# Differential-attention q and k stored in rows of four and loaded as one DMA of 128 rows; Hyena with its own buffers for both parts, its loads issued first, its pointwise work on VectorE alone

## The chip, the cores and the metric

The kernel runs on one core of one Trainium2 chip. Its time is the device time of one execution in microseconds (us). Three runs of the kernel before lie between 4696.3 and 4708.67, with a median of 4706.38.

## The reference

Two backbone layers work on a trunk of 1024 latent tokens and 256 context tokens, 1024 channels, everything in fp32. A layer is: adaLN RMSNorm, one input projection whose columns go to four head groups, the four mixers, concatenation and output projection with a gated residual, then a squared-ReLU MLP. The context stream is needed after layer 0 only, so layer 1 computes the output for the latent tokens alone. The four mixers are gated DeltaNet (a chunked recurrence), Hyena, HGRN2 (a chunked recurrence with vector gates) and differential attention. Two of them are touched here:

```python
def hyena_mixer(...):                       # per stream: 1024 latent tokens, 256 context tokens (layer 0 only)
    v, x1, x2 = _split(conv_centred(t, conv_w), [W_GROUP] * 3)
    z = x1 * long_conv_bidir(v, h_fwd0, h_bwd0, skip[0])     # order 0; a convolution by FFT over 2n
    return x2 * long_conv_bidir(z, h_fwd1, h_bwd1, skip[1])  # order 1
# differential attention: two softmax maps per head over q, k of 32 channels each
# out = (softmax(q1 k1) - lam * softmax(q2 k2)) @ v, then a sub-norm
```

## The kernel before, in words

**Stages of a layer.** Norm; projection (TensorE bound) with the DeltaNet woven in; HGRN2 with the end of the projection and the start of Hyena woven in; attention with the rest of Hyena, the modulation vectors (`mods`) and, in layer 0, the filters of layer 1 woven in; then the tail (output projection and MLP), which is almost all TensorE. The weaving is done by Python generators: `mix(lead, fill)` takes a step of the lead (HGRN2 in `hgrn`, later attention), which yields its size, and then as many steps of the fill (`rest`) as that size pays for. What comes earlier in that order has priority; a planner then orders each engine's instructions by priority among those that its own clock thinks ready. Each engine, and the queue SP that issues nearly all DMAs, runs its list strictly in order. A tile with one buffer can be written again only when all readers of the old contents are done, and a new memory pool waits for the readers of what lay at its place.

**Where Hyena starts.** `rest` (inside `run`) ends the projection, frees the pools on the right side of the memory (normed activations, weights, projection temporaries), opens attention's pool, issues the q and k loads of the first head (`next(at[0])`, L1157), issues the first two loads of modulation weights (`next(m2)`, L341), and only then starts `hyena`, whose first loads are its own (L1446 to L1458, the DFT bases through `basis`, L1311). All of that is issued before HGRN2's next tile (`hg_tile`) issues its loads (L1033 to L1041).

**Hyena.** The long convolution is done as two DFTs by matmul. In layer 0 the part "c" (256 context tokens, radix R = 2, one block, a = 1) runs first and then the part "l" (1024 latent tokens, R = 4, a = 2); in layer 1 only "l". Input `u` (yv), gate `xg` (y1 or y2) and spectrum `ks` have one buffer each for both parts, as large as "l" needs. For each order `od`, `u` is transposed (`put`, L1468, TensorE), transformed (`pF`, L1317), multiplied with the spectrum (L1504 to L1509) between radix butterflies (L1497 to L1502 and L1515 to L1525), and transformed back (`py`, L1532) into `u`. Of these pointwise instructions, 6 of an "l" block and 1 of a "c" block go to GpSimd (`G`), the others to VectorE (`V`), with two extra tiles `t1` and `t2`.

**q and k of attention.** They are kept in two halves, a high and a low part that add up to the fp32 value, so that a product needs pairs of parts. `post_d` writes [part, channel, group, token] to scratch, one DMA for each chunk of 512 or 256 tokens, from the tile `dhl` that has one buffer (L654 to L657). `load` in `attn` fills, for each of two maps of a head, 128 partitions for q (high, low, high, low of 32 channels) and 128 for k (high, high, low, low) by two DMAs of 64 partitions each: eight per head, 320 KB each (256 KB for q in layer 1). The heads 1 to 3 are loaded two query tiles into the head before.

Of the kernel before, what the change touches and what calls it, by code (L numbers as in the profile page):

```python
# [9 lines left out]
F32 = mybir.dt.float32  # L10
# [10 lines left out]
CTX = 256  # L21
# [219 lines left out]
class K:  # L241
# [185 lines left out]
    def scratch(self, l):  # L427
        S = self.S = {}
        for n in CM_COL:
            if n in ("hf", "hb"):  # L430
                S["k" + n] = self.dram(f"k{n}_{l}", [128, 2, T])
                S["l" + n] = self.dram(f"l{n}_{l}", [128, T // 64, 2, 2, 64])
            elif n in ("dq", "dk"):
                S[n] = self.dram(f"{n}_{l}", [2, 128, 2, T])
            elif n[0] != "g":
                S[n] = self.dram(f"{n}_{l}", [128, 2, T])
        g = self.dram(f"g_{l}", [128, 6, T])
        S["gk"], S["gv"], S["gq"] = [g[:, 2 * j:2 * j + 2] for j in range(3)]
        for n in list(S):
            for i in range(2):  # L440
                S[n, i] = S[n][:, :, i] if n in ("lhf", "lhb", "dq", "dk") else S[n][:, i]
        S["g"] = g
        for n, a, w in TM:
            S[n] = self.dram(f"{n}_{l}", [128, NT, w])
        for k in range(KT):
            S["o", k] = self.dram(f"o{k}_{l}", [128, T])
# [190 lines left out]
    def post_d(self, l, tp, name, i, u, a, n):  # L637
        nc = self.nc
        u = u[:, a:a + n]
        r = self.inv_norm(tp, u, self.c["bones32"], 1.0 / 32, 32 * EPS)  # L640
        y = self.e(tp, 2, n)
        nw = self.P["dqw" if name == "dq" else "dkw"]
        nc.vector.scalar_tensor_tensor(y, u, nw, r, ALU.mult, ALU.mult)
        if a < SEQ:

            rc, rs = self.e(tp, 1, n), self.e(tp, 3, n)
            nc.sync.dma_start(rc, self.i["c_rcos"][:, a:a + n])
            nc.sync.dma_start(rs, self.i["c_rsin"][:, a:a + n])
            t2 = self.e(tp, 0, n)
            p = self.aux("prope")  # L650
            nc.tensor.matmul(p[:, :n], self.c["rperm"], y, start=True, stop=True)
            nc.vector.tensor_mul(t2, p[:, :n], rs)
            nc.vector.tensor_mul(y, y, rc)
            nc.vector.tensor_add(y, y, t2)  # L654
        hl = tp.tile([128, 2, 512], F32R, tag="lf", name="dhl", bufs=1)
        self.split(hl[:, 0, :n], hl[:, 1, :n], y, lo_eng=nc.vector)
        nc.sync.dma_start(self.S[name, i][:, :, a:a + n].rearrange("x p t -> p x t"), hl[:, :, :n].bitcast(F32))  # L657


    def gdn(self, l):  # L660
# [476 lines left out]
    def attn(self, l, qp):  # L1137
# [8 lines left out]
        def load(i, b):  # L1146

            out = ops[i, b] = []
            for j in range(2):
                r = slice(64 * b + 32 * j, 64 * b + 32 * j + 32)  # L1150
                for nm, n in (("q", 128 * NQ), ("k", T)):
                    t = pools[heads.index((i, b)) % 2].tile([128, T], F32R, tag=f"{nm}{j}", name=f"{nm}{j}")[:, :n]
                    raw = t.bitcast(F32)
                    src = S["d" + nm, i]
                    for x in range(2):
                        v = src[:, r, :n] if nm == "q" else src[x:x + 1, r, :n].to_broadcast([2, 32, n])
                        nc.sync.dma_start(raw[64 * x:64 * x + 64], v)  # L1157
                    out.append(t)

        pools = [qp]  # L1160
# [280 lines left out]
    def hyena(self, l):  # L1441
# [2 lines left out]
        gp = es.enter_context(tc.tile_pool(name=f"hy{l}", bufs=1, side="right", reuse_waits="tile"))  # L1444
        sk = gp.tile([128, 4], F32, tag="sk", name="sk")
        nc.sync.dma_start(sk, self.i["hysk"][l])  # L1446
        V, G = nc.vector, nc.gpsimd
        for nm, tok0, n, a, R in (("c", SEQ, CTX, 1, 2), ("l", 0, SEQ, 2, 4)):
            if (l, nm) not in self.KS:
                continue  # L1450
            tk = slice(tok0, tok0 + n)
            pn = n // R
            bf, bi = self.basis(gp, "f", nm), self.basis(gp, "i", nm)
            u = gp.tile([128, 2, SEQ], F32, tag="u", name="u")[:, :, :n]
            nc.sync.dma_start(u, S["yv"][:, :, tk])
            for od in range(2):
                xg = gp.tile([128, 2, SEQ], F32, tag="xg", name="xg")[:, :, :n]
                nc.sync.dma_start(xg, S["y1" if od == 0 else "y2"][:, :, tk])  # L1458

                ut = gp.tile([128, 2, 4, 256], F32, tag="ut", name="ut")  # L1460
                for ai in range(a):
# [8 lines left out]
                        nc.scalar.copy(ut[:, ai, b0:b0 + 2], pv)  # L1470
                        yield 0.2
                for k in range(a):
                    ks = gp.tile([128, 4, 2, 256], F32, tag="ks", name="ks")[:, :R]
                    nc.sync.dma_start(ks, self.KS[l, nm][:, od, k])
                    X = gp.tile([128, 4, 2, 256], F32, tag="X", name="X")[:, :R]
                    Y = gp.tile([128, 4, 2, 256], F32, tag="Y", name="Y")[:, :R]
                    t1 = gp.tile([128, 4, 256], F32, tag="t1", name="t1")[:, :R]
                    t2 = gp.tile([128, 4, 256], F32, tag="t2", name="t2")[:, :R]

                    def F(b):  # L1480
                        p = self.big("pF").rearrange("p (r c) -> p r c", r=2)
                        for ri in range(2):
                            self.fourier(bf, ut, a, ri, k, b, p[:, ri])
                        return p
                    Z = X
                    if R == 2:
                        nc.scalar.copy(Y[:, 0], F(0))
                        p = F(1)
                        V.tensor_add(X[:, 0], Y[:, 0], p)
                        V.tensor_sub(X[:, 1], Y[:, 0], p)  # L1490
                    else:
                        for b in range(2):
                            nc.scalar.copy(X[:, b], F(b))
                            p = F(b + 2)
                            V.tensor_add(Y[:, 2 * b], X[:, b], p)
                            V.tensor_sub(Y[:, 2 * b + 1], X[:, b], p)
                        G.tensor_add(X[:, 0], Y[:, 0], Y[:, 2])  # L1497
                        V.tensor_sub(X[:, 2], Y[:, 0], Y[:, 2])
                        V.tensor_add(X[:, 1, 0], Y[:, 1, 0], Y[:, 3, 1])
                        V.tensor_sub(X[:, 1, 1], Y[:, 1, 1], Y[:, 3, 0])  # L1500
                        G.tensor_sub(X[:, 3, 0], Y[:, 1, 0], Y[:, 3, 1])
                        G.tensor_add(X[:, 3, 1], Y[:, 1, 1], Y[:, 3, 0])  # L1502
                    yield 1
                    V.tensor_mul(t1, X[:, :, 0], ks[:, :, 0])  # L1504
                    G.tensor_mul(t2, X[:, :, 1], ks[:, :, 1])
                    V.tensor_mul(Y[:, :, 1], X[:, :, 0], ks[:, :, 1])
                    V.tensor_mul(X[:, :, 0], X[:, :, 1], ks[:, :, 0])
                    V.tensor_sub(Y[:, :, 0], t1, t2)
                    V.tensor_add(Y[:, :, 1], Y[:, :, 1], X[:, :, 0])  # L1509
                    if R == 2:  # L1510
                        V.tensor_add(Z[:, 0], Y[:, 0], Y[:, 1])
                        V.tensor_sub(Z[:, 1], Y[:, 0], Y[:, 1])
                    else:
                        c = [t.rearrange("p a c -> p (a c)").rearrange("p (s r c) -> p s r c", s=2, r=2) for t in (t1, t2)]
                        V.tensor_add(c[0][:, 0], Y[:, 0], Y[:, 2])  # L1515
                        G.tensor_add(c[1][:, 0], Y[:, 1], Y[:, 3])
                        V.tensor_sub(c[0][:, 1], Y[:, 0], Y[:, 2])
                        V.tensor_sub(c[1][:, 1], Y[:, 1], Y[:, 3])
                        c1, d1 = c[0][:, 1], c[1][:, 1]
                        G.tensor_add(Z[:, 0], c[0][:, 0], c[1][:, 0])  # L1520
                        V.tensor_sub(Z[:, 2], c[0][:, 0], c[1][:, 0])
                        V.tensor_sub(Z[:, 1, 0], c1[:, 0], d1[:, 1])
                        V.tensor_add(Z[:, 1, 1], c1[:, 1], d1[:, 0])
                        V.tensor_add(Z[:, 3, 0], c1[:, 0], d1[:, 1])
                        V.tensor_sub(Z[:, 3, 1], c1[:, 1], d1[:, 0])  # L1525
# [197 lines left out]
    def run(self):  # L1723
        nc, tc = self.nc, self.tc
        with ExitStack() as es:
# [4 lines left out]
            for l in range(DEPTH):  # L1730
# [10 lines left out]
                with ExitStack() as ls:  # L1741
# [42 lines left out]
                    def rest():  # L1784
                        yield from project
                        rs.close()
                        at.append(self.attn(l, qs.enter_context(pool("daf", side="right"))))
                        next(at[0])
                        with pool("mods", side="right") as mp:
                            m2 = self.mods(l, range(16, 48), mp)  # L1790
                            next(m2)
                            yield from weave(self.hyena(l), m2, RM[l])
                            if full:
                                yield from self.mods(l + 1, range(16), mp)
                        if full:
                            yield from self.filters(l + 1)
# [58 lines left out]
```

## Time and profile before

| | |
|---|---|
| median of three runs | 4706.38 us |
| the profiled execution, its own time | 4706.21 us |
| its span, first to last instruction | 4704.4 us |
| TensorE busy, VectorE busy, GpSimd busy | 4081.9, 2352.6, 1082.8 us |
| mean granted TensorE clock | 0.915 of full speed |

The durations in the rows come from the one profiled execution. A busy time is the sum of an engine's instructions; idle time in front of an instruction stands in square brackets with what ended it. The two layers stand one after the other: HGRN2, attention and Hyena of layer 0 lie from about 750 to 1560 us and those of layer 1 from about 3200 to 3890 us.

### The profile page before, as it was taken

Reading aid. Unit: us, or ns where it says so; the run is one execution under the profiler, and the core shown is the slowest. Engines: PE = TensorE matmul, PEld = TensorE weight load, DVE = VectorE, ACT = ScalarE, POOL = GpSimd, SP = SyncE. Lnnn points to the kernel's source line nnn. Section 1 sums busy time; section 2 is a strip of 40 time slices with the busy share of each in tenths; the row PEclk is TensorE's granted clock in tenths of the full one; section 3 lists DMA queues with packets and bytes.
Section 4 is the critical chain, followed back from the end, with each engine's and each line's share of the span. In section 5 each row is a group of like instructions: output and inputs, shape, how many; then the busy total and the mean of one; then the engine's idle time right before and its main releaser. Section 6 shows DMA issues by size and latency. Waiting matters only on the chain. (4 is left out here: it accounts for less than half of the span.)

```text
span 4704.4 us, 81485 instructions
## 1 busy us (share of the span) xinstructions
PE 4081.9 (87%) x33270; PEld 3290.9 (70%) x33270; DVE 2352.6 (50%) x4599; ACT 1620.4 (34%) x3165; POOL 1082.8 (23%) x1101
## 2 busy tenths in 40 slices
PE   4987999867477799999999987999847788999999
PEld 2866877655355588888888776776635667888887
DVE  7566556647587353222222756456647874322222
ACT  3453413423245342212122554514313464321222
POOL 1121110000121344333333221120001114433333
PEclk7998999877789899999999998899867899999999
DMA  5236633224324421111111326634342234111112
GB/s 194 87 89 169 199 97 111 92 91 145 97 84 147 156 79 50 36 41 36 41 36 49 118 82 159 184 107 124 97 143 71 84 113 145 64 48 49 46 49 88
DMA packets 381355, 458.61 MB, mean 97 GB/s; under 512 B 137108, under 2 KB 244244, under 8 KB 378933
## 3 DMA queue, kind: packets, MB, share of 16 engines
q1 hardware_dynamic: 379156, 448.42, 30.4%
q0 software_dynamic: 1824, 4.98, 0.4%
q8 instruction: 262, 4.29, 0.4%
q14 instruction: 113, 0.92, 0.1%
HBM read 343.81 MB, written 109.48 MB: 96 GB/s over the span
## 5 line engine op out<-in xcount | busy, mean ns | idle before, releaser
L255 POOL TENSOR_TENSOR wlo<-wraw,whi 128x512 fp32r<-128x512 f32 x360 | 478.3, 1334 | 743.3 <-ACT whi L254 739.2
L254 ACT CAST whi<-wraw 128x512 fp32r<-128x512 f32 (+1 forms) x480 | 296.5, 619 | 905.4 <-PE pt L260 757.4
L1597 DVE SCALAR_TENSOR_TENSOR tx<-pt,mod,tx 128x512 f32<-128x512 f32 (+1 forms) x360 | 250.6, 696 | 590.6 <-PE pt L261 590.5
L260 PE MATMUL pt<-fl,whi 128*128 128x512 f32 (+1 forms) x1280 | 475.4, 371 | 0.0
L261 PE MATMUL pt<-fh,wlo 128*128 128x512 f32 (+1 forms) x1280 | 475.4, 371 | 0.0
L259 PE MATMUL pt<-fh,whi 128*128 128x512 f32 (+1 forms) x1280 | 475.1, 371 | 0.0
L261 PE MATMUL pt<-hh,wlo 128*128 128x512 f32 (+1 forms) x1280 | 471.2, 368 | 2.8 <-POOL wlo L255 2.8
L260 PE MATMUL pt<-hl,whi 128*128 128x512 f32 (+1 forms) x1280 | 471.9, 369 | 0.0
L259 PE MATMUL pt<-hh,whi 128*128 128x512 f32 (+1 forms) x1280 | 471.2, 368 | 0.4 <-ACT f L1630 0.4
L1631 DVE TENSOR_TENSOR f<-f 128x512 f32<-128x512 f32 (+1 forms) x160 | 149.3, 935 | 622.9 <-ACT f L1630 619.2
L259 PE MATMUL pproj<-hh,whi 128*128 128x512 f32 (+1 forms) x960 | 372.0, 387 | 7.0 <-ACT u L487 6.4
L260 PE MATMUL pproj<-hl,whi 128*128 128x512 f32 (+1 forms) x960 | 362.0, 377 | 0.0
L261 PE MATMUL pproj<-hh,wlo 128*128 128x512 f32 (+1 forms) x960 | 360.6, 376 | 0.0
L255 POOL TENSOR_TENSOR fl<-f,fh 128x512 fp32r<-128x512 f32 (+1 forms) x160 | 191.5, 1198 | 390.6 <-ACT fh L254 387.0
L260 PEld LDWEIGHTS pt<-fl,whi 128*128 128x128 f32 x1280 | 240.1, 188 | 47.3 <-issue 0.2
L261 PEld LDWEIGHTS pt<-fh,wlo 128*128 128x128 f32 x1280 | 240.1, 188 | 47.1 <-issue 0.5
L259 PEld LDWEIGHTS pt<-fh,whi 128*128 128x128 f32 x1280 | 240.1, 188 | 47.0 <-ACT whi L254 0.2
L261 PEld LDWEIGHTS pt<-hh,wlo 128*128 128x128 f32 x1280 | 241.3, 188 | 44.3 <-POOL wlo L255 4.1
L259 PEld LDWEIGHTS pt<-hh,whi 128*128 128x128 f32 x1280 | 241.3, 189 | 41.0 <-ACT f L1630 0.8
L260 PEld LDWEIGHTS pt<-hl,whi 128*128 128x128 f32 x1280 | 241.3, 189 | 40.3 <-issue 0.2
L259 PEld LDWEIGHTS pproj<-hh,whi 128*128 128x128 f32 x960 | 186.5, 194 | 47.1 <-ACT u L487 8.2
L1199 ACT ACTIVATE p<-psc,mx 128x1280 f32<-128x1280 f32 (+1 forms) x144 | 178.0, 1238 | 120.0 <-DVE mx L1198 71.1
(380 smaller groups left out, 8330.7 us busy)
## 6 DMA issues: line engine op xcount, KB each, us to landing
wraw<-mlp_w SPq DMA_DIRECT2D x296, 256.0 KB
modw<-mod_w SPq DMA_DIRECT2D x80, 512.0 KB
wraw<-w_cm SPq DMA_DIRECT2D x88, 256.0 KB
wraw<-w_out SPq DMA_DIRECT2D x64, 256.0 KB
kv<-kvd SPq DMA_DIRECT2D x40, 256.0 KB
k<-dk SPq DMA_DIRECT2D x32, 320.0 KB
bfl<-c_hyfl SPq DMA_DIRECT2D x4, 2048.0 KB
modw<-mod_w SPq DMA_DIRECT2D x4, 2048.0 KB
```

Source lines behind the costliest of these rows:

```text
L254: (hi_eng or nc.scalar.copy)(hi, src)
L255: (lo_eng or nc.gpsimd).tensor_tensor(lo, src, hi.bitcast(F32), ALU.subtract)
L259: nc.tensor.matmul(ps, wh, xh, start=start, stop=False)
L260: nc.tensor.matmul(ps, wh, xl, start=False, stop=False)
L261: nc.tensor.matmul(ps, wl, xh, start=False, stop=stop)
L1199: nc.scalar.activation(p[j], A, AF.Exp, bias=mx[:, j:j + 1], accum_out=sm[:, j:j + 1])
L1597: nc.vector.scalar_tensor_tensor(xm, p, G[:, m, v:v + 1], xm, ALU.mult, ALU.add)
L1631: nc.vector.tensor_mul(f, f, f)
```

## The change

q and k scratch has the layout [group, channel, 4, token]. `post_d` writes each chunk by two DMAs from the same tile, so that every channel has its four rows in the order in which the tile wants them (q: high, low, high, low; k: high, high, low, low). The load of one map of one head is then one DMA of 32 channels times 4 rows = 128 rows: four per head.

`hyena` has tiles of their own for the two parts (`uc`, `ul`, `xgc`, `xgl`, `ksc`, `ksl`), issues all first loads of both parts before its first `yield 0`, and loads only later spectra and gates in the loop. `rest` starts Hyena's loads first, then attention's, then those of the modulation weights, and yields 1.0 before Hyena's work. No instruction of Hyena is left on GpSimd; `t1` and `t2` are gone and the products are made in `X` and `Y`; two butterfly pairs are joined into instructions of twice the length.

```diff
-                S[n] = self.dram(f"{n}_{l}", [2, 128, 2, T])
+                S[n] = self.dram(f"{n}_{l}", [2, 128, 4, T])
...
-        nc.sync.dma_start(self.S[name, i][:, :, a:a + n].rearrange("x p t -> p x t"), hl[:, :, :n].bitcast(F32))
+        for d in range(2):
+            rows = slice(2 * d, 2 * d + 2) if name == "dq" else slice(d, 4, 2)
+            nc.sync.dma_start(self.S[name, i][:, rows, a:a + n], hl[:, :, :n].bitcast(F32))
...
-                    raw = t.bitcast(F32)
-                    src = S["d" + nm, i]
-                    for x in range(2):
-                        v = src[:, r, :n] if nm == "q" else src[x:x + 1, r, :n].to_broadcast([2, 32, n])
-                        nc.sync.dma_start(raw[64 * x:64 * x + 64], v)
+                    c0 = 64 * b + 32 * j
+                    nc.sync.dma_start(t.bitcast(F32), S["d" + nm, i][c0:c0 + 32, :, :n].rearrange("c r t -> (c r) t"))
...
+        got = {}
+        for nm, tok0, n, a, R in parts:
+            bf = self.basis(gp, "f", nm)
+            u = gp.tile([128, 2, n], F32, tag="u" + nm, name="u")
+            nc.sync.dma_start(u, S["yv"][:, :, tok0:tok0 + n])
+            ks = spectrum(nm, 0, 0, R)
+            bi = self.basis(gp, "i", nm)
+            got[nm] = bf, bi, u, gate(nm, 0, tok0, n), ks
+        yield 0
...
-                        G.tensor_add(X[:, 0], Y[:, 0], Y[:, 2])
+                        V.tensor_add(X[:, 0], Y[:, 0], Y[:, 2])
...
-                        G.tensor_sub(X[:, 3, 0], Y[:, 1, 0], Y[:, 3, 1])
-                        G.tensor_add(X[:, 3, 1], Y[:, 1, 1], Y[:, 3, 0])
+                        V.tensor_sub(X[:, 3, 0], Y[:, 1, 0], Y[:, 3, 1])
+                        V.tensor_add(X[:, 3, 1], Y[:, 1, 1], Y[:, 3, 0])
...
-                    V.tensor_mul(t1, X[:, :, 0], ks[:, :, 0])
-                    G.tensor_mul(t2, X[:, :, 1], ks[:, :, 1])
+                    V.tensor_mul(Y[:, :, 0], X[:, :, 0], ks[:, :, 0])
                     V.tensor_mul(Y[:, :, 1], X[:, :, 0], ks[:, :, 1])
-                    V.tensor_mul(X[:, :, 0], X[:, :, 1], ks[:, :, 0])
-                    V.tensor_sub(Y[:, :, 0], t1, t2)
-                    V.tensor_add(Y[:, :, 1], Y[:, :, 1], X[:, :, 0])
+                    V.tensor_mul(X[:, :, 0], X[:, :, 1], ks[:, :, 1])
+                    V.tensor_mul(X[:, :, 1], X[:, :, 1], ks[:, :, 0])
+                    V.tensor_sub(Y[:, :, 0], Y[:, :, 0], X[:, :, 0])
+                    V.tensor_add(Y[:, :, 1], Y[:, :, 1], X[:, :, 1])
...
-                        V.tensor_add(c[0][:, 0], Y[:, 0], Y[:, 2])
-                        G.tensor_add(c[1][:, 0], Y[:, 1], Y[:, 3])
-                        V.tensor_sub(c[0][:, 1], Y[:, 0], Y[:, 2])
-                        V.tensor_sub(c[1][:, 1], Y[:, 1], Y[:, 3])
-                        c1, d1 = c[0][:, 1], c[1][:, 1]
-                        G.tensor_add(Z[:, 0], c[0][:, 0], c[1][:, 0])
-                        V.tensor_sub(Z[:, 2], c[0][:, 0], c[1][:, 0])
+                        Z = Y
+                        V.tensor_add(X[:, 0:2], Y[:, 0:2], Y[:, 2:4])
+                        V.tensor_sub(X[:, 2:4], Y[:, 0:2], Y[:, 2:4])
+                        V.tensor_add(Z[:, 0], X[:, 0], X[:, 1])
+                        V.tensor_sub(Z[:, 2], X[:, 0], X[:, 1])
+                        c1, d1 = X[:, 2], X[:, 3]
...
-                        next(at[0])
                         with pool("mods", side="right") as mp:
-                            m2 = self.mods(l, range(16, 48), mp)
-                            next(m2)
-                            yield from weave(self.hyena(l), m2, RM[l])
+                            hy, m2 = self.hyena(l), self.mods(l, range(16, 48), mp)
+                            for g in (hy, at[0], m2):
+                                next(g)
+                            yield 1.0
+                            yield from weave(hy, m2, RM[l])
```

## Rows read from the trace of the kernel before

**Rows 1.** The page: busy time of each engine, and the DMA traffic of the span.
```profile
PE 4081.9 (87%) x33270; PEld 3290.9 (70%) x33270; DVE 2352.6 (50%) x4599; ACT 1620.4 (34%) x3165; POOL 1082.8 (23%) x1101
...
DMA packets 381355, 458.61 MB, mean 97 GB/s; under 512 B 137108, under 2 KB 244244, under 8 KB 378933
```
**Rows 2.** Timeline of TensorE, layer 0: start, duration, line, tiles, [idle before <-releaser].
```profile
1062.32 1.13 PE L1468 MATMUL put<-c_ident,u 128*128 128x128 f32 x4 [32.60 <-DMA u<-yv]
...
1210.34 1.96 PE L1468 MATMUL put<-c_ident,u 128*128 128x128 f32 x8 [34.41 <-DMA u<-yv]
```
**Rows 3.** Waits of TensorE, 3395 to 3900: total us, times, longest.
```profile
PE put L1468 <- DMA u<-yv: 46.5, 1, 46.5
...
PE pmod L363 <- DMA modw<-mod_w: 7.2, 1, 7.2
```
**Rows 4.** The queue SP in layer 1: start, time that the issue took, line.
```profile
3411.82 0.55 SPq L1157 DMA_DIRECT2D q<-dq  x1
...
3429.15 11.38 SPq L1157 DMA_DIRECT2D k<-dk  x2
...
3454.25 2.32 SPq L1455 DMA_DIRECT2D u<-yv  x1
...
3470.75 0.52 SPq L1036 DMA_DIRECT2D k<-khb  x1
```
**Rows 5.** Stretches: busy us of each engine, granted clock, DMA share, GB/s.
```profile
820.00:975.00 155.00, 133.13 (x2179) 99.25 (x2178) 96.99 (x265) 64.77 (x140) 2.70 (x7) 0.87 0.31 98
...
3415.00:3445.00 30.00, 18.92 (x342) 13.29 (x330) 11.66 (x36) 8.62 (x20) 0.37 (x2) 0.60 0.14 52
3455.00:3475.00 20.00, 0.00 (x0) 0.00 (x0) 0.00 (x0) 0.00 (x0) 0.00 (x0) 0.50 1.00 301
3475.00:3485.00 10.00, 0.00 (x0) 0.00 (x0) 0.00 (x0) 0.00 (x0) 0.00 (x0) 0.50 0.15 58
20.00:45.00 25.00, 15.50 (x67) 4.94 (x67) 18.65 (x33) 4.08 (x7) 2.95 (x3) 0.80 1.04 396
```
**Rows 6.** The queue SP in layer 0, as rows 4.
```profile
1000.25 0.52 SPq L1157 DMA_DIRECT2D q<-dq  x1
...
1203.91 0.58 SPq L1455 DMA_DIRECT2D u<-yv  x1
```
**Rows 7.** Timeline of VectorE behind the first waits of the layers.
```profile
1067.15 0.69 DVE L1489 TENSOR_TENSOR X<-Y,pF 128x512 f32<-128x512 f32 x1 [2.33 <-PE pF L1317]
...
1070.82 0.41 DVE L1061 TENSOR_TENSOR X<-X,k 128x256 f32<-128x256 f32 x1
...
3488.37 0.43 DVE L1061 TENSOR_TENSOR X<-X,k 128x256 f32<-128x256 f32 x1 [0.42 <-DMA k<-khb]
```
**Rows 8.** VectorE by line and shape: busy us, mean ns | idle before.
```profile
L1506 DVE TENSOR_TENSOR Y<-X,ks 128x1024 f32<-128x1024 f32 x8 | 17.7, 2218 | 0.0
...
L1518 DVE TENSOR_TENSOR t<-Y 128x512 f32<-128x512 f32 x8 | 11.2, 1397 | 0.0
...
L1498 DVE TENSOR_TENSOR X<-Y 128x512 f32<-128x512 f32 x8 | 10.9, 1360 | 0.0
L1496 DVE TENSOR_TENSOR Y<-X,pF 128x512 f32<-128x512 f32 x16 | 10.9, 680 | 0.0
L1508 DVE TENSOR_TENSOR Y<-t,t 128x1024 f32<-128x1024 f32 x8 | 9.7, 1211 | 0.0
...
L1515 DVE TENSOR_TENSOR t<-Y 128x512 f32<-128x512 f32 x8 | 8.3, 1032 | 0.0
...
L1499 DVE TENSOR_TENSOR X<-Y 128x256 f32<-128x256 f32 x8 | 7.5, 938 | 0.0
...
L1523 DVE TENSOR_TENSOR X<-t,t 128x256 f32<-128x256 f32 x8 | 3.3, 412 | 0.0
```
**Rows 9.** The queue SP in the projection, layer 0, as rows 4.
```profile
835.80 4.34 SPq L657 DMA_DIRECT2D dk<-dhl  x2
```

More of the change, by code (lines that the diff above doesn't have):

```diff
@@ L440, in scratch @@
             for i in range(2):
-                S[n, i] = S[n][:, :, i] if n in ("lhf", "lhb", "dq", "dk") else S[n][:, i]
+                S[n, i] = S[n][:, :, i] if n in ("lhf", "lhb") else S[n][i] if n in ("dq", "dk") else S[n][:, i]
         S["g"] = g
@@ L1149, in load @@
             for j in range(2):
-                r = slice(64 * b + 32 * j, 64 * b + 32 * j + 32)
                 for nm, n in (("q", 128 * NQ), ("k", T)):
                     t = pools[heads.index((i, b)) % 2].tile([128, T], F32R, tag=f"{nm}{j}", name=f"{nm}{j}")[:, :n]
-                    raw = t.bitcast(F32)
-                    src = S["d" + nm, i]
-                    for x in range(2):
-                        v = src[:, r, :n] if nm == "q" else src[x:x + 1, r, :n].to_broadcast([2, 32, n])
-                        nc.sync.dma_start(raw[64 * x:64 * x + 64], v)
+                    c0 = 64 * b + 32 * j
+                    nc.sync.dma_start(t.bitcast(F32), S["d" + nm, i][c0:c0 + 32, :, :n].rearrange("c r t -> (c r) t"))
                     out.append(t)
@@ L1446, in hyena, with gate, spectrum @@
         nc.sync.dma_start(sk, self.i["hysk"][l])
[L1447 to L1450, printed above, removed]
+        V = nc.vector
+        parts = [p for p in (("c", SEQ, CTX, 1, 2), ("l", 0, SEQ, 2, 4)) if (l, p[0]) in self.KS]
+        def gate(nm, od, tok0, n):
+            xg = gp.tile([128, 2, n], F32, tag="xg" + nm, name="xg")
+            nc.sync.dma_start(xg, S["y1" if od == 0 else "y2"][:, :, tok0:tok0 + n])
+            return xg
+        def spectrum(nm, od, k, R):
+            ks = gp.tile([128, R, 2, 256], F32, tag="ks" + nm, name="ks")
+            nc.sync.dma_start(ks, self.KS[l, nm][:, od, k])
+            return ks
+        got = {}
[7 more added lines that the diff above has]
+        yield 0
+        for nm, tok0, n, a, R in parts:
             tk = slice(tok0, tok0 + n)
             pn = n // R
-            bf, bi = self.basis(gp, "f", nm), self.basis(gp, "i", nm)
-            u = gp.tile([128, 2, SEQ], F32, tag="u", name="u")[:, :, :n]
-            nc.sync.dma_start(u, S["yv"][:, :, tk])
+            bf, bi, u, xg, ks = got[nm]
             for od in range(2):
-                xg = gp.tile([128, 2, SEQ], F32, tag="xg", name="xg")[:, :, :n]
-                nc.sync.dma_start(xg, S["y1" if od == 0 else "y2"][:, :, tk])
+                if od:
+                    xg = gate(nm, od, tok0, n)
                 ut = gp.tile([128, 2, 4, 256], F32, tag="ut", name="ut")
@@ L1472, in hyena @@
                 for k in range(a):
-                    ks = gp.tile([128, 4, 2, 256], F32, tag="ks", name="ks")[:, :R]
-                    nc.sync.dma_start(ks, self.KS[l, nm][:, od, k])
+                    if od or k:
+                        ks = spectrum(nm, od, k, R)
                     X = gp.tile([128, 4, 2, 256], F32, tag="X", name="X")[:, :R]
                     Y = gp.tile([128, 4, 2, 256], F32, tag="Y", name="Y")[:, :R]
-                    t1 = gp.tile([128, 4, 256], F32, tag="t1", name="t1")[:, :R]
-                    t2 = gp.tile([128, 4, 256], F32, tag="t2", name="t2")[:, :R]
                     def F(b):
@@ L1484, in F @@
                         return p
-                    Z = X
                     if R == 2:
@@ L1500, in hyena @@
                         V.tensor_sub(X[:, 1, 1], Y[:, 1, 1], Y[:, 3, 0])
-                        G.tensor_sub(X[:, 3, 0], Y[:, 1, 0], Y[:, 3, 1])
-                        G.tensor_add(X[:, 3, 1], Y[:, 1, 1], Y[:, 3, 0])
+                        V.tensor_sub(X[:, 3, 0], Y[:, 1, 0], Y[:, 3, 1])
+                        V.tensor_add(X[:, 3, 1], Y[:, 1, 1], Y[:, 3, 0])
                     yield 1
-                    V.tensor_mul(t1, X[:, :, 0], ks[:, :, 0])
-                    G.tensor_mul(t2, X[:, :, 1], ks[:, :, 1])
+                    V.tensor_mul(Y[:, :, 0], X[:, :, 0], ks[:, :, 0])
                     V.tensor_mul(Y[:, :, 1], X[:, :, 0], ks[:, :, 1])
-                    V.tensor_mul(X[:, :, 0], X[:, :, 1], ks[:, :, 0])
-                    V.tensor_sub(Y[:, :, 0], t1, t2)
-                    V.tensor_add(Y[:, :, 1], Y[:, :, 1], X[:, :, 0])
+                    V.tensor_mul(X[:, :, 0], X[:, :, 1], ks[:, :, 1])
+                    V.tensor_mul(X[:, :, 1], X[:, :, 1], ks[:, :, 0])
+                    V.tensor_sub(Y[:, :, 0], Y[:, :, 0], X[:, :, 0])
+                    V.tensor_add(Y[:, :, 1], Y[:, :, 1], X[:, :, 1])
                     if R == 2:
+                        Z = X
                         V.tensor_add(Z[:, 0], Y[:, 0], Y[:, 1])
@@ L1513, in hyena @@
                     else:
-                        c = [t.rearrange("p a c -> p (a c)").rearrange("p (s r c) -> p s r c", s=2, r=2) for t in (t1, t2)]
-                        V.tensor_add(c[0][:, 0], Y[:, 0], Y[:, 2])
-                        G.tensor_add(c[1][:, 0], Y[:, 1], Y[:, 3])
-                        V.tensor_sub(c[0][:, 1], Y[:, 0], Y[:, 2])
-                        V.tensor_sub(c[1][:, 1], Y[:, 1], Y[:, 3])
-                        c1, d1 = c[0][:, 1], c[1][:, 1]
-                        G.tensor_add(Z[:, 0], c[0][:, 0], c[1][:, 0])
-                        V.tensor_sub(Z[:, 2], c[0][:, 0], c[1][:, 0])
+                        Z = Y
[4 more added lines that the diff above has]
+                        c1, d1 = X[:, 2], X[:, 3]
                         V.tensor_sub(Z[:, 1, 0], c1[:, 0], d1[:, 1])
```

## The prediction, written before the changed kernel was run

> **What bounds the kernel now.** I read the page first: TensorE is busy for 4081.9 of 4704.4 us, VectorE for half of them, and the DMA moves 97 GB/s in the mean [rows 1]. TensorE sets the end, so what can be won is where it stands idle. The waits of TensorE in the stretches that the change touches, HGRN2 to attention, come next: one releaser stands above all others, the load of Hyena's input `u`. TensorE waits for it for 32.6 and 34.4 us in layer 0 [rows 2] and 46.5 us in layer 1 [rows 3], 113.5 us in all. TensorE runs its list in order, so HGRN2 or attention, which come behind `put`, stand too: the multiplications of HGRN2's next tile begin on VectorE at 1070.8 and 3488.4 us [rows 7].
>
> Why `u` is late is read from the queue SP and the DMA share. In layer 1 the eight loads of q and k start at 3411.8 us; the last two alone hold SP for 11.4 us, and `u` is issued at 3454.3 us, HGRN2's next `k` at 3470.8 us [rows 4]. From 3415 to 3445 the DMA share is 0.14 at 52 GB/s: some 2 of 16 engines work (0.14 x 16 = 2.2), at 26 GB/s each. Then the wide transfers come, 1.00 and 301 GB/s, and at the end again 0.15 [rows 5]: the two engines that had q and k still have their share of everything issued behind to do, and `u` is complete only with them. So the loads of q and k are slow, they hold the queue, and they delay what comes behind them even after it has been issued. The second wait of layer 0 has one cause more: `u` of part "l" shares its buffer with part "c" and is issued only at 1203.9 us [rows 6], when "c" has been written out.
>
> **Part 1: q and k as 128 rows.** Removed: 32 of 64 load DMAs. The nearest rows for a transfer of 128 rows are the stretches with all engines at work, 301 GB/s (the modulation weights with their short rows among them) and 396 GB/s (activations) [rows 5]. One head in layer 0 is 4 x 640 KB = 2.62 MB: 6.6 to 8.7 us in place of some 45 us of the two engines (2.62 MB at 58 GB/s). [...]
>
> For heads 1 to 3 the transfers lie beside attention, where VectorE is the busier engine, and I cost them at the one wait that they show: 7.2 us for a modulation weight behind q and k [rows 3]. The other end is 0, if that weight is late anyway.
>
> **Part 2: writing four rows.** Added: 22 DMAs of up to 512 KB, 10.0 MB in all, in the projections, where the DMA share is 0.31 [rows 5]; bandwidth hides them. The cost is `dhl`: with one buffer, the next chunk's cast on ScalarE, and what stands behind it there (the copies that empty PSUM for TensorE), waits until both writes are read out. A second write takes its issue and 1.7 us of transfer (512 KB at 301 GB/s), 2.1 us x 22 = 46 us if every one is on the path; two issues with one chunk's wait between them took 4.34 us [rows 9]. No engine waits for these writes now, and the chunks mostly come further apart than that, so I take 4 us. Ends 0 and 46.
>
> **Part 3: own buffers, loads first.** Moved: six loads in layer 1, eleven in layer 0, in front of q and k and of two modulation loads on SP; those of "l" in layer 0 also in front of HGRN2's loads of several tiles. By the tiles' sizes (1 MB here is 10^6 bytes), layer 1 issues 7.34 MB for Hyena, 2.36 MB of q and k, 1.05 MB of modulation weights: 10.75 MB. Layer 0 has 1.57 MB for "c" and the larger q and k as well: 12.58 MB. Hyena's own wait is gone, since its first 3.1 MB (basis and `u`) take 10 us while TensorE still has work. What is late next is HGRN2's next `k`, which stands behind all of this, as it did before.
> - Layer 1: 3411.8 + 10.75 / 0.301 = 3447.5 in place of 3488.4: **40.9 us** [rows 4, 5, 7].
> - Layer 0, first wait: 1000.25 + 12.58 / 0.301 = 1042.1 in place of 1070.8, 28.7 us [rows 5 to 7]. VectorE had done Hyena's first four instructions between 1067.15 and 1070.82 [rows 7], which now come later: less 3.7 us, **25.0 us**.
> - Layer 0, second wait: `u` of "l" has landed long before and nothing else is missing: all of it, **34.4 us**.
>
> I take 301 GB/s because modulation weights are in both; at 396 the first two give 49.4 and 34.8 us less 3.7, 14.7 us more in all (layer 1: 27.1 us, layer 0: 31.8 us of transfer). At the mean of the span see the rivals.
>
> The `yield 1.0` moves one step of fill behind attention in each layer. Layer 1 ends Hyena well before attention, so nothing; in layer 0 the filters of layer 1 already run on after attention, and one step more alone there costs between 0 and some 20 us. I take 3.
>
> **Part 4: no GpSimd.** Undisturbed, 512 elements take VectorE 0.68 us, 1024 take 1.21 and 256 take 0.41 [rows 8]. An "l" block gains instructions of 512 (butterfly), 2 x 256, 1024 (product), one in the inverse butterfly (0.68), and two pairs of 0.68 there, of which three were VectorE's, become two of 1.21 (+0.38): 0.68 + 0.82 + 1.21 + 0.68 + 0.38 = 3.8 us; 8 blocks are 30 us, and two of "c" 1.4. Against that, those that ran beside GpSimd are stretched: L1506 2.22 in place of 1.21, L1518 1.40, L1498 1.36 and L1515 1.03 in place of 0.68, L1499 and its twin 0.94 in place of 0.41 [rows 8]: 1.01 + 0.72 + 0.68 + 0.35 + 1.06 = 3.8 us a block, 31 us. Net +1 us. The ends: +31 if the stretching stays, -10 if VectorE's other instructions and the waits for GpSimd's results gain too. The cover matters, because VectorE is the busier engine in these stretches.
>
> **Sum.** 40.9 + 25.0 + 34.4 + 7.2 = 107.5 us, less 4 + 3 + 1 = 8: 99.5 us. The profiled execution took 4706.2 us, within 0.2 us of the median, so 4706.2 - 99.5 = **4606.7, forecast 4607**.
>
> **The rivals.**
> - A, the forecast: 0.70, its own range 4580 to 4640.
> - B, the second write of each chunk is on the path: 46 us in place of 4, 4649. For it: one buffer, engines in order. Against: DMA share 0.31 and no such wait now. 0.11.
> - C, the change doesn't do what it says, and the new loads of q and k still sit on two engines. Hyena no longer waits, but HGRN2's `k` does: in layer 1 each of the two has 1.18 MB and a sixteenth of 8.39 MB, 1.70 MB at 26 GB/s = 65.5 us, 3477.3: 11 us gained. In layer 0 1.31 + 0.62 MB, 74 us: 7 us lost with the 3.7. With 34.4 and less 8, 30 us: 4676. Against: both sides now lead with 32 or 128. 0.06.
> - D, slower: the block of 10.75 and 12.58 MB in front of HGRN2's loads becomes the wait. At r GB/s it gains 76.6 - 10750 / r in layer 1 and 66.9 - 12580 / r in layer 0, and 34.4 + 7.2 - 8 besides: 177 - 23330 / r, which turns negative below 132 GB/s. At the 97 GB/s of the span [rows 1] it is -63.5 us, 4770. For it: TensorE's list now has HGRN2's tile in front of Hyena's work, so nothing fills the hole. Against: 301 and 396 GB/s where much is queued [rows 5]. 0.06.
> - E, more than forecast: the transfers at 396 GB/s and VectorE freed of 10 us, 4607 - 14.7 - 11 = 4581, and some clock regained (it was granted at half speed in the waits [rows 5]): below 4570 in 0.07.
>
> **How the numbers follow.** The range is 4566 to 4664: it holds A, E's better part and B, and leaves out C, D and some of E. A measurement can't tell less than 0.3% (14 us) from no change. All of A, B, E and nearly all of C are faster by more; a mix of B, C and D's mild form is the same. Faster 0.92, same 0.02, slower 0.06.
>
> **What would show it.** Right: no wait of TensorE for `u<-yv` over 5 us; a DMA share near 1 for 25 to 40 us from the first q and k loads; HGRN2's next multiplication 40 us (layer 1) and 25 to 30 us (layer 0) earlier against the end of the projection; L1506's successor at 1.2 us. Wrong: a share of 0.13 during q and k (C), ScalarE's cast waiting for `dk<-dhl` (B), a wait of HGRN2 for `k` or `lf` longer than 15 us (D), VectorE instructions in Hyena still stretched (part 4).

## The result and the profile after

The changed kernel takes 4598.77 us (median of four runs, 4594.1 to 4605.16), the kernel before, timed beside it, 4704.45: a ratio of 0.9779, 95% interval 0.9766 to 0.9792. The forecast was 4607, faster. The profiled execution took 4594.1 us with a span of 4592.3 us; the granted clock rose from 0.915 to 0.925 in the mean.

The page of the kernel after, to be held against [rows 1]: TensorE's busy time is the same within 3 us, so all but 3 of the 112 us of span that went are idle time. The four rows cost 10 MB of DMA traffic.
```profile
PE 4079.2 (89%) x33270; PEld 3286.2 (72%) x33270; DVE 2336.7 (51%) x4633; ACT 1617.3 (35%) x3165; POOL 1006.1 (22%) x1051
...
DMA packets 387720, 468.56 MB, mean 102 GB/s; under 512 B 137843, under 2 KB 246515, under 8 KB 385300
```
The transposes `put` in the kernel after, by tile, with what TensorE sat idle for before them. The 113.5 us of [rows 2, 3] have become 0.4.
```profile
L1484 PE MATMUL put<-c_ident,u x72: 275/285/489, 1014.2 to 3560.5; 128*128 128x128 f32 x72
its engine sat idle before it (us, times) until:
  ACT wT L1220: 0.9, 2
  DMA u<-yv: 0.4, 1
```
The queue SP of the kernel after in layer 1, which answers to [rows 4]. The four loads of q and k take 0.3 to 0.6 us each where two of before held SP for 11.4 us, and HGRN2's `k` is issued 14 us after the projection's last write (L535), where it was 57 us before (3413.4 to 3470.75). Between the two pairs stand Hyena's loads (3353.2 to 3357.1): although the code asks for Hyena's loads first, the first pair of q and k still goes ahead of them. The line by itself below them is the projection's last write in the kernel before.
```profile
3350.76 0.32 SPq L1156 DMA_DIRECT2D q<-dq  x1
3352.35 0.32 SPq L535 DMA_DIRECT2D v<-tm  x1
3352.76 0.39 SPq L1156 DMA_DIRECT2D k<-dk  x1
...
3357.69 0.60 SPq L1156 DMA_DIRECT2D q<-dq  x1
3358.65 0.33 SPq L1156 DMA_DIRECT2D k<-dk  x1
3359.02 4.87 SPq L341 DMA_DIRECT2D modw<-mod_w  x2
3366.78 0.52 SPq L1039 DMA_DIRECT2D k<-khb  x1
```

```profile
3413.41 0.32 SPq L534 DMA_DIRECT2D v<-tm  x1
```
The stretches that answer to those of q and k in [rows 5], after: busy us of each engine, granted clock, DMA share, GB/s. The block runs at a share of 1.00 and 400 GB/s while TensorE works beside it.
```profile
1020.00:1040.00 20.00, 14.92 (x296) 11.20 (x296) 6.55 (x23) 4.02 (x9) 0.19 (x1) 0.59 1.00 400
...
3360.00:3380.00 20.00, 17.23 (x280) 12.29 (x280) 7.21 (x21) 7.48 (x18) 0.19 (x1) 0.50 1.00 409
```
VectorE after, at HGRN2's next multiplication of each layer, to be held against [rows 7].
```profile
1041.37 0.41 DVE L1064 TENSOR_TENSOR X<-X,k 128x256 f32<-128x256 f32 x1
...
1044.31 0.69 DVE L1502 TENSOR_TENSOR X<-Y,pF 128x512 f32<-128x512 f32 x1 [1.52 <-PE pF L1316]
...
3382.58 0.42 DVE L1064 TENSOR_TENSOR X<-X,k 128x256 f32<-128x256 f32 x1 [0.20 <-DMA k<-khb]
```
And VectorE by line and shape after, against [rows 8]: nothing in Hyena's pointwise work is stretched any more (L1511 here is L1498 there, L1512 is L1499).
```profile
L1518 DVE TENSOR_TENSOR Y<-X,ks 128x1024 f32<-128x1024 f32 x8 | 9.7, 1217 | 0.0
...
L1511 DVE TENSOR_TENSOR X<-Y 128x512 f32<-128x512 f32 x8 | 5.5, 683 | 0.0
...
L1512 DVE TENSOR_TENSOR X<-Y 128x256 f32<-128x256 f32 x8 | 3.3, 417 | 0.0
```

Where the time went, by fixed points of both traces (starts on the queue and on TensorE, us from the span's start; `psc` are attention's scores, `pfin` the transposes that end HGRN2, `pt` the products of the tail):

| stretch | before | after | gained |
|---|---|---|---|
| start to the projection's last write, layer 0 | 999.9 | 1005.8 | -5.9 |
| to attention's first `psc` (HGRN2) | 137.8 | 106.1 | 31.7 |
| to the first `pt` of the tail (attention, Hyena, filters) | 483.4 | 454.0 | 29.4 |
| to the projection's last write, layer 1 | 1792.3 | 1786.5 | 5.8 |
| to the last `pfin` (HGRN2) | 171.8 | 127.6 | 44.2 |
| to the last `psc` (attention) | 281.6 | 269.8 | 11.8 |
| to the last `pt` of the tail | 833.5 | 838.4 | -4.9 |

The gains sum to 112.1 us, which are the 112 us of the spans. The medians differ by 105.7.

### The profile page after: what moved, and what is told of

Read it like the earlier page. It is cut to its first block, busy times and chain, and to the rows that moved or that the text cites. A ratio compares the mean times of both kernels' runs of the same rounds, so it can differ in the third digit from the quotient of the medians.

```text
span 4592.3 us, 81385 instructions
## 1 busy us (share of the span) xinstructions
PE 4079.2 (89%) x33270; PEld 3286.2 (72%) x33270; DVE 2336.7 (51%) x4633; ACT 1617.3 (35%) x3165; POOL 1006.1 (22%) x1051
```

## The experiments

In all of them the ratio is to the kernel before, timed on the same chip beside them.

**q and k alone (e1_qk).** The kernel before with the changed scratch, the doubled writes and the loads of 128 rows, and nothing else of the change.
```diff
-                    for x in range(2):
-                        v = src[:, r, :n] if nm == "q" else src[x:x + 1, r, :n].to_broadcast([2, 32, n])
-                        nc.sync.dma_start(raw[64 * x:64 * x + 64], v)
+                    nc.sync.dma_start(t.bitcast(F32), S["d" + nm, i][c0:c0 + 32, :, :n].rearrange("c r t -> (c r) t"))
```


> The kernel before with the q and k part alone (rows of four, two writes a chunk, one load of 128 rows); Hyena, its order and GpSimd as before. Theory (the two engines are the main cause): in layer 0, 2.62 + 1.05 + 1.05 MB before the gate land in 16 us, in layer 1 9.7 MB in 32 us, so both first waits of TensorE for u shrink to under 8 us; in the second wait of layer 0, u is still issued after part c has been written out, and some 10 of 34 us stay. 4704 - 30 - 42 - 23 - 7 + 6 = about 4608 us, no later than 4625. Rival (order and shared buffers are the main cause): the waits for u stay above 20 us each and the time is 4650 us or more.

Measured: 4585.54 us, ratio 0.973 (0.9702 to 0.9757). This one part brings more than the whole change, and 22 us more than the theory's 4608. `u` still has its one buffer and stands behind q, k and the modulation weights, and yet no wait for it is left. The transposes of this kernel, by tile:
```profile
L1466 PE MATMUL put<-c_ident,u x72: 271/283/465, 1029.6 to 3532.7; 128*128 128x128 f32 x72
its engine sat idle before it (us, times) until:
  ACT wT L1219: 0.5, 1
  ACT ut L1468: 0.4, 2
```

**All but q and k (e2_loads).** The changed kernel with scratch, writes and loads of q and k as before.
```diff
-                    nc.sync.dma_start(t.bitcast(F32), S["d" + nm, i][c0:c0 + 32, :, :n].rearrange("c r t -> (c r) t"))
+                    for x in range(2):
+                        v = src[:, r, :n] if nm == "q" else src[x:x + 1, r, :n].to_broadcast([2, 32, n])
+                        nc.sync.dma_start(raw[64 * x:64 * x + 64], v)
```


> The changed kernel with q and k as before (one write a chunk, eight loads of 64 rows a head); Hyena's own buffers, loads first and no GpSimd stay. Theory (the two engines are the main cause): Hyena no longer waits for u, but HGRN2's next k stands behind q and k on the two engines until 3477 us in layer 1 and 1074 us in layer 0, as it did before; what is gained is the second wait of layer 0 (34 us) and 10 us besides: 4655 to 4675 us. Rival (order and buffers are the main cause): 4620 us or less.

Measured: 4734.58 us, ratio 1.0051 (1.0033 to 1.007): half a per cent slower than before, which neither theory allowed. Hyena's loads now stand ahead of most of q and k, and `u` is still waited for by 15.0 us in layer 0; above all, TensorE waits for what comes last instead, the modulation weights behind q and k. Its waits in layer 0 (990 to 1650) and its queue SP:
```profile
PE pmod L363 <- DMA modw<-mod_w: 72.3, 10, 37.9
...
PE put L1485 <- DMA u<-yv: 15.0, 1, 15.0
```
```profile
1022.09 5.18 SPq L1157 DMA_DIRECT2D k<-dk  x2
1027.31 17.32 SPq L1157 DMA_DIRECT2D q<-dq  x2
1044.68 12.33 SPq L1157 DMA_DIRECT2D k<-dk  x2
1057.05 6.02 SPq L341 DMA_DIRECT2D modw<-mod_w  x1
```
These loads of q and k hold the queue for 35 us (5.2 + 17.3 + 12.3), and the wait has only changed its name: 37.9 us at one `pmod` in layer 0, 37.7 at one in layer 1. Own buffers and early loads do not remove a wait that slow transfers cause. This kernel has the yield too, which costs some 19 to 26 us in the pairs below; how much of its loss is the yield's, no run tells.

**The pointwise work alone (e3_nopool).** The kernel before with Hyena's pointwise instructions on VectorE, made in `X` and `Y`.
```diff
-                    V.tensor_mul(t1, X[:, :, 0], ks[:, :, 0])
-                    G.tensor_mul(t2, X[:, :, 1], ks[:, :, 1])
+                    V.tensor_mul(Y[:, :, 0], X[:, :, 0], ks[:, :, 0])
...
+                    V.tensor_mul(X[:, :, 0], X[:, :, 1], ks[:, :, 1])
```


> The kernel before with the pointwise work of Hyena alone changed (all on VectorE, in place, joined pairs). Theory: VectorE's 31 us more of instructions and 31 us less of stretching cancel: 4700 to 4710 us, with each 1024-element product at 1.21 us. Rival 1: VectorE is the bound there and the added work shows: 4720 us or more. Rival 2: other instructions gain as well: 4690 us or less.

Measured: ratio 0.9986 (0.9972 to 0.9999), 4704.69 us; most likely a gain of 7 us, between 0 and 13 by the interval, hardly told from none.

**Hyena's loads last (e4_last).**
```diff
-                            for g in (hy, at[0], m2):
+                            for g in (at[0], m2, hy):
```


> The changed kernel with the order of the first loads turned round: attention's q and k, then the modulation weights, then Hyena's. Theory: with all engines at work the order no longer matters, since u and the basis still land some 20 us after the first issue, before TensorE runs out of work: within 8 us of the changed kernel's 4599. Rival (loads first is what counts): TensorE waits again for u in front of its first transposes, over 10 us in each layer: 4615 to 4640 us.

Measured: 4597.98 us, ratio 0.9758 (0.9732 to 0.9783). The order of the loads is worth nothing that can be told once q and k are wide.

**Two halves that do not lead with 2 (e5_halves).** The change, with each load cut into two of 64 partitions, 16 channels times 4 rows each, joined into one dimension of 64 rows.
```diff
-                    nc.sync.dma_start(t.bitcast(F32), S["d" + nm, i][c0:c0 + 32, :, :n].rearrange("c r t -> (c r) t"))
+                    for x in range(2):
+                        c1 = c0 + 16 * x
+                        nc.sync.dma_start(t[64 * x:64 * x + 64].bitcast(F32), S["d" + nm, i][c1:c1 + 16, :, :n].rearrange("c r t -> (c r) t"))
```


> The changed kernel with each load of q or k cut into two DMAs of 64 rows (16 channels of four rows each), with a leading dimension of 16 or more instead of the 2 of the kernel before. Theory (the short leading dimension held them on two engines): same time as the changed kernel, 4593 to 4606 us, DMA share near 1 during q and k. Rival (it is the joining of two halves that counts): back to a share near 0.14 and 4650 us or more.

Measured: 4613.38 us, ratio 0.9802 (0.9779 to 0.9826), some 15 us over the change by the medians (11 by the ratios, whose intervals overlap) and 7 over the upper end of the theory, far from the 4650 of the rival. The windows of this kernel, columns as in [rows 5]:
```profile
1000.00:1020.00 20.00, 12.15 (x281) 9.64 (x279) 8.30 (x30) 5.61 (x14) 0.39 (x1) 0.76 0.87 300
1020.00:1040.00 20.00, 12.86 (x270) 9.17 (x268) 6.32 (x22) 4.03 (x9) 0.19 (x1) 0.59 1.03 309
```
Halves as such are not confined to few engines; halves that lead with 2 are. The Trainium skill ("DMA: Bandwidth & Descriptors", section "Rules for kernel authors") says that an outermost dimension of fewer than 16 confines a DMA to at most that many engines. The trace agrees: a leading dimension of 2 left the share at 0.14 [rows 5], and the halves of 64 rows brought it to 1.03. The same section says that two transfers to disjoint halves of the partitions both spread over all 16 engines. That agrees with the halves here (1.03) and not with those of the kernel before (0.14), where the measurement decides.

Most of what remains can be seen as waits for the modulation weights, which stand behind twice as many issues: 15.1 us in layer 0 where the change has 4.5, and 9.3 in layer 1 where it has 1.4.

**Four loads of 32 rows, single write (e6_rows32).** The change with the scratch and the single write of before; each tile is filled by four DMAs of 32 channels.
```diff
+                    for m, x in enumerate((0, 1, 0, 1) if nm == "q" else (0, 0, 1, 1)):
+                        nc.sync.dma_start(raw[32 * m:32 * m + 32], src[x, r, :n])
```


> The changed kernel with the scratch and the single write of a chunk as before, and each map of a head loaded by four DMAs of 32 rows (one part each) instead of one of 128: sixteen issues a head. Theory (leading dimension, and the doubled write costs some 6 us in the projection of layer 0): 4590 to 4600 us, the end of the projection in layer 0 back at 1000 us. Rival 1 (32 rows at a time are slow, or sixteen issues hold the queue): 4610 to 4640 us. Rival 2 (the doubled write costs nothing): 4599 us.

Measured: 4615.96 us, ratio 0.9808 (0.9784 to 0.9833), in the range of the first rival, though its interval overlaps that of the change. The projection of layer 0 ends at 998.2 us where that of the change ends at 1005.8, so the second write seems to cost something there (the mean over all traces is taken below); but four loads of `k` in a row held SP for 10.8 us, the weights were late by 10.1 us, and TensorE was busy for only 7.5 of the 20 us from 1020 to 1040.
```profile
1008.31 10.82 SPq L1156 DMA_DIRECT2D k<-dk  x4
```

**Without the yield (e7_noyield).**
```diff
-                            yield 1.0
```


> The changed kernel without the yield of 1.0 behind the first loads, so that Hyena's first transposes come one step of HGRN2 earlier in the order. Theory: one step of fill less runs alone after attention in layer 0: 0 to 6 us faster, 4593 to 4599. Rival (the step keeps TensorE from waiting for u, or HGRN2 from being held back): TensorE waits for u by 5 to 15 us in a layer and the time is 4605 to 4620.

Measured: 4572.6 us, ratio 0.9713 (0.969 to 0.9737): 26 us faster than the change, where six were the most that was expected. The inverse transform of Hyena's part "l" in layer 0 begins 16 us earlier than in the change (1173.4 for 1189.1), and the last filter multiplication ends the stage 23 us earlier. Counted from the projection's last write, which itself came 3 us earlier, these are 12 and 20 us. The filter multiplications of layer 1 that are woven into layer 0, by tile, from 1400 to 1600 us, first in the change, then in the kernel without the yield:
```profile
L1396 PE MATMUL pw<-wh,h2l x16: 468/696/1096, 1486.3 to 1542.7; 128*128 128x512 f32 x16
```
```profile
L1396 PE MATMUL pw<-wh,h2l x16: 467/700/796, 1460.5 to 1519.5; 128*128 128x512 f32 x16
```
Attention itself ends before that (its last `psc` is at 1468.4 and 1452.8 us), so in layer 0 the fill ends last, and what puts the fill off puts the tail off.

**GpSimd put back (e8_gp).** The change with the six instructions per "l" block and the one per "c" block on GpSimd again, in place.
```diff
-                        V.tensor_add(X[:, 0], Y[:, 0], Y[:, 2])
+                        G.tensor_add(X[:, 0], Y[:, 0], Y[:, 2])
...
-                    V.tensor_mul(X[:, :, 0], X[:, :, 1], ks[:, :, 1])
+                    G.tensor_mul(X[:, :, 0], X[:, :, 1], ks[:, :, 1])
```


> The changed kernel with six instructions of each l block and one of each c block put back on GpSimd, in place as they are now (they run beside VectorE and stretch it). Theory (added work and stretching cancel): 4594 to 4606 us, VectorE instructions beside GpSimd stretched again to 1.4 to 2.2 us, the waits of TensorE for Hyena's products as long as now. Rival 1: GpSimd off is worth something: 4610 us or more. Rival 2: VectorE is the bound: 4585 us or less.

Measured: 4610.47 us, ratio 0.9795 (0.9772 to 0.9819): 12 us more by the medians, at the lower end of the first rival, though the ratio's interval overlaps that of the change. VectorE's instructions are stretched as in [rows 8], and one of them now waits for GpSimd's product:
```profile
L1511 DVE TENSOR_TENSOR X<-Y 128x512 f32<-128x512 f32 x8 | 11.2, 1402 | 0.0
...
L1520 DVE TENSOR_TENSOR X<-X,ks 128x1024 f32<-128x1024 f32 x8 | 9.8, 1223 | 7.5 <-POOL X L1519 7.5
```

**q and k with the pointwise work (e9_qk_pw).** The edits of e1_qk and e3_nopool together: shared buffers, old order, no yield.

> The kernel before with the rows of four for q and k and the pointwise work on VectorE alone: shared buffers, the old order of loads, no yield. It and the change without its yield (4572.6 us) differ in the own buffers and the order of the loads alone. Theory (those are worth nothing once q and k are wide): 4572, within 8 us. Rival (the 13 us between q and k alone, 4585.5, and the change without its yield come from own buffers and early loads, part 4 gives nothing): 4580 to 4590.

Measured: 4565.57 us, ratio 0.9705 (0.9684 to 0.9726), the best of all, and the same as the change without its yield (0.9713). Those two differ in own buffers and early loads alone, so these are worth nothing here. This holds for the second wait of layer 0 too, where `u` of "l" shares its buffer with "c". The queue SP of this kernel there, and below it that of the kernel before:
```profile
1114.08 0.43 SPq L1155 DMA_DIRECT2D q<-dq  x1
1114.55 0.65 SPq L1155 DMA_DIRECT2D k<-dk  x1
1124.38 0.32 SPq L1537 DMA_DIRECT2D o<-u  x1
...
1135.41 0.32 SPq L1537 DMA_DIRECT2D o<-u  x1
...
1137.17 0.57 SPq L1453 DMA_DIRECT2D u<-yv  x1
```
```profile
1150.95 12.36 SPq L1157 DMA_DIRECT2D q<-dq  x2
1163.35 12.07 SPq L1157 DMA_DIRECT2D k<-dk  x2
1175.53 0.38 SPq L1542 DMA_DIRECT2D o<-u  x1
...
1184.47 1.47 SPq L1542 DMA_DIRECT2D o<-u  x1
...
1203.91 0.58 SPq L1455 DMA_DIRECT2D u<-yv  x1
```
In the kernel before, the second head's q and k hold the queue in front of the writes of "c", and weights and `u` follow behind. In e9_qk_pw the four loads take under 2 us together, `u` is issued at 1137.2 us, and TensorE waits 0.4 us for it:
```profile
PE put L1466 <- DMA u<-yv: 0.4, 1, 0.4
```

**The yield alone (e10_qk_yield).** e1_qk with one line more.
```diff
+                            yield 1.0
                             yield from weave(self.hyena(l), m2, RM[l])
```


> The kernel before with the rows of four for q and k (4585.5 us alone) and one line more, the yield of 1.0 ahead of Hyena. Theory (one step of the fill moved behind HGRN2's and attention's steps costs some 26 us by itself, in layer 0, because the fill ends last there): 4605 to 4620, with the end of the filters of layer 1 and the first inverse transform of the part l some 20 us later than with q and k alone. Rival (the yield costs only in the company of the early loads, which it keeps apart from their use): 4580 to 4592.

Measured: 4604.45 us, ratio 0.9787 (0.9765 to 0.9809): 19 us more than without, just under the lower end of the theory and 12 over the rival. The filters end 13 us later (1537.6 for 1524.1), the first inverse transform of "l" comes 10 us later (1180.3 for 1170.4); counted from the projection's last write, 18 and 15 us. The yield costs by itself, with no early loads beside it.

**Twice the yield (e11_yield2).**
```diff
-                            yield 1.0
+                            yield 2.0
```


> The change with yield 2.0 in place of yield 1.0. Theory (each unit sends one step more of the lead ahead of Hyena, at about the same price): 26 us more than the change, some 4625, between 4612 and 4640. Rival 1 (the price is that of the first gap only): 4592 to 4606. Rival 2 (the lead's step is larger than 2, so that nothing is moved but the debt): within 5 us of the change as well, but with the same first inverse transform of the part l as in the change, 1189 us.

Measured: 4592.14 us, ratio 0.9757 (0.9738 to 0.9776), the first rival: no more than with 1.0, rather some less, though the intervals overlap. The second rival wanted the first inverse transform of "l" at 1189 us; it comes at 1180.4. So the price is not so much per step. What both yields share is a stretch in which TensorE waits for VectorE's butterfly in front of `py`: 38.9 us in layer 0 of the change, 41.7 with 2.0, 28.5 without; the pair above has 24.8 with the yield and 10.5 without. The inverse transforms of "l" by tile (1140 to 1400), the change and then the kernel without the yield:
```profile
L1545 PE MATMUL py<-bil,Y x128: 379/379/767, 1189.1 to 1376.4; 128*128 128x256 f32 x128
...
  DVE Y L1533: 38.9, 4
```
```profile
L1545 PE MATMUL py<-bil,Y x128: 377/379/792, 1173.4 to 1350.1; 128*128 128x256 f32 x128
...
  DVE Y L1533: 28.5, 4
```

## Why the prediction was right, and where it was not

**The cause.** Right: the 113.5 us of waits for `u` came from q and k on a few engines, two by the share. The share during q and k rose from 0.14 to near 1 (rival C fell), and e1_qk shows that this edit alone takes the waits away.

**Part 1.** The step that failed: it was credited with 7.2 us, and part 3 with 100.3. e1_qk and e2_loads turn that round. Part 1 alone, with the doubled writes of part 2 in it, gives 127 us by its ratio (0.027 of 4705) and 119 against the first timing of the kernel before (4704.5 less 4585.5), and all else without it is 0.5% slower. The prediction gave the cause in its first paragraphs, and then booked the gain to the edit that moves the waiting load, at the rate that only part 1 brings. Rival C shows that this was half known: with q and k still slow it left 30 of the 99.5 us, at 4676. e2_loads, which is nearly that kernel, takes 4734.6: C looked at HGRN2's `k` alone and not at the modulation weights behind q and k (37.9 and 37.7 us), and it booked the yield at 3. The attention of layer 1 gained 11.8 us, against 7.2.

**Part 2.** The mean end of the projection of layer 0 in the nine traces with doubled writes is 1003.6 us, in the four with single writes 999.6: 4 us in layer 0 (the single ends lie from 998.2 to 1000.9, the doubled from 1000.3 to 1006.5), where 4 were taken for both layers. No wait of ScalarE for `dk<-dhl` appears, and rival B fell; two writes issued together take SP 1.2 us, not 4.3 as in [rows 9].
```profile
827.51 1.22 SPq L660 DMA_DIRECT2D dk<-dhl  x2
```

**Part 3, the terms.** From the projection's last write, HGRN2's next multiplication moved by 44.8 us in layer 1 (75.0 to 30.2), against 40.9; the stretch gained 44.2. In layer 0 it moved by 35.4 (71.0 to 35.6) against 25 to 30, and the stretch gained 31.7 against 25.0. The rate was sized too low: I took 301 GB/s, and the trace has 400 and 409. At 396 the prediction's terms come to 49.4 and 35.1: its "34.8 us less 3.7" is a slip, since 70.6 (1070.8 less 1000.25) less 31.8 is 38.8, so that rate was worth 18.6 us and not 14.7, and E's sum is 4577. No wait of HGRN2 for `k` over 1 us followed, so rival D fell. The second wait of layer 0 is gone with all its 34.4 us, but not for the reason given: the prediction named the shared buffer, and e9_qk_pw has that buffer and no wait. It had read the line of `u` at 1203.9 us and not the loads of q and k in front of it on the same queue.

**The yield.** Sized at 3 us with ends 0 and 20; by the medians it costs 26 us in the change and 19 in e10_qk_yield (20.5 and 15.4 by the profiled spans). The prediction saw that the filters run on alone behind attention in layer 0 and still took the low end. Of the 29.4 us that the stretch of attention and filters gained in layer 0, the wait gave 34.4 and the yield took 17 (the stretch is 454.0 us in the change and 436.9, from 1105.9 to 1542.8, without it), so other things gave some 12. Part 4 and, as in layer 1, the later heads that no longer hold the queue are candidates; how they share it was not measured.

**Part 4.** Sized at a loss of 1, with -10 as one end; it gains 7 to 12 us (e3_nopool, e8_gp, and 0.973 to 0.9705 from e1_qk to e9_qk_pw), at that end or just beyond it, though each interval leaves room for next to nothing. The sum of the stretched rows left out three, L1504 at 1418 ns, L1517 at 813 and L1522 at 495, some 3.4 us over eight blocks. VectorE's busy time fell by 15.9 us though it has taken over GpSimd's instructions, and the wait for GpSimd's product that e8_gp shows, 7.5 us, is not there. The rows of the "l" blocks make 3.4 us of the 15.9 (151.3 before, 147.9 after); the rest lies in other lines.

So 4607 came out close because gains sized too small (the rate, part 4, what the later heads held up) and a loss sized too small (the yield) cancelled; in so far the number is luck. What stays open is how the yield costs what it costs: one unit and two cost about the same, and the traces show a displaced fill with more waits for VectorE, but no experiment here told which step's displacement does it.

## What to carry to other kernels

When a load is late, read the whole queue in front of it and the DMA share, and look for the transfer whose leading dimension is short: cure that one before buffers or order, which here only gave the wait another name. Before adding a step in front of a woven stage, look which of the two, lead or fill, ends last: where the fill does, as here, putting it off puts off the end of the stage (18 to 20 us in layer 0, for a step sized at 3). And a bundle of edits is worth taking apart even when it wins: here two of its edits beat the whole by 0.7%.

## What the runs showed of the hardware

- Transfers issued behind a DMA that sits on two engines are late with it: in e2_loads one modulation weight was waited for 37.9 us in layer 0, with a DMA share of 0.37 from 1060 to 1080, and one for 37.7 us in layer 1, with 0.13 from 3470 to 3490. A share of 0.13 is that of two engines out of 16; that the weights are complete only when these two have caught up is read from it and not seen engine by engine.
```profile
1060.00:1080.00 20.00, 0.00 (x0) 0.00 (x0) 0.00 (x0) 0.00 (x0) 0.00 (x0) 0.50 0.37 118
...
3470.00:3490.00 20.00, 1.27 (x3) 0.45 (x2) 0.00 (x0) 2.06 (x4) 0.19 (x1) 0.59 0.13 51
```
- The number of issues seems to count even where the share is near 1: the same bytes of q and k in twice as many DMAs cost 15 us by the medians (e5_halves), and in four times as many 17 us with the second write taken away (e6_rows32); by the ratios the intervals overlap that of the change.
- A subtraction of 512 elements on VectorE (L1511) takes 1.40 us in e8_gp, where GpSimd works beside it, and 0.68 in the change, where it does not.
